# Attention scores from a stacked query by two full-height products, and the second layer's S5 parameter steps started one expert later at a lower rank

## The chip, the cores and the metric

One Trainium2 chip, one core of it. The metric is the time of one execution on the device in microseconds (us); each kernel is run several times and the median is used. The engines are named as in the profile: PE (matrix products and transposes), DVE (vector), ACT (scalar), POOL (GpSimd), and SP, which only issues DMAs here; ACT issues some too.

## What is computed

Two layers of a hybrid backbone on a latent stream of 512 tokens and a context of 256, width 1024. Each layer is a mixer of four branches (attention, SSD, S5, short convolution), merged by gates, and then a mixture of 16 experts in which every expert picks its tokens (64 of the latent stream, 32 of the context). The second layer returns the latent stream alone. The two places that the change touches:

```
def gqa_attend(q, k, v):              # 8 query heads, 2 key heads, head size 64
    qg = q.reshape(b, T, G, H // G, d)
    s = jnp.einsum('btgrd,bsgd->bgrts', qg, k) * (d ** -0.5)
    p = jax.nn.softmax(s, axis=-1)
    o = jnp.einsum('bgrts,bsgd->btgrd', p, v)

def s5_discretise(lam_re, lam_im, log_step, b_re, b_im):
    step = jnp.exp(log_step)[:, None]
    mag = jnp.exp(lr * step)
    ab_re, ab_im = mag * jnp.cos(li * step), mag * jnp.sin(li * step)
    ...
    bb_re = coef_re[..., None] * br - coef_im[..., None] * bi
```

The S5 parameters of a layer (powers of the complex transition, and from them small matrices per group of channels) depend on weights alone, not on the tokens.

## The kernel before, in words

The program is written stage by stage; a scheduler puts each engine's instructions in one fixed order by estimated times and by a priority that follows the order of the code. Each engine then runs its own list strictly in that order, and waits where an operand or a buffer isn't ready.

**Precision.** Many products are made from pairs: `split_to` (L113 to L115) writes a float32 array as a rounded high part (ACT, L114) and a remainder (DVE, L115), and `mm3` (L99 to L101) adds three products: high by high, low by high, high by low.

**Attention** (L861 on). For k and for two groups of four query heads, a projection of 256 columns is made, rotated and normalised into `R` (128 tokens, tile, head, 64). Then `R` is transposed by PE (L925): two query heads side by side make a block of 128 columns, so one transpose serves two heads; a key head is first copied twice side by side into `kd` by DVE (L921). The results go to the pairs `qT` and `kT` (H and L), in which head 0 of a pair holds rows 0 to 63 and head 1 rows 64 to 127. `scores` (L929) runs once for each tile of 128 tokens and each of four head pairs: for two pieces of 384 keys and two heads one `mm3` of 64 rows, that is 12 products, into banks `psb` (three of the four) and `psa`; then maximum (DVE), exponential (ACT, L949) and scaling. `values` transposes the probabilities (L963) and multiplies by V (L968). In the first layer the two context tiles take part too, with one piece of 256 keys. The scheduler fills PE between these with products `psmm` of other stages (gates, modulation), which are due later anyway.

**Experts** (L1500 to L1660). Tokens are gathered by DMA (`xg`), transposed (PE, L1493), scaled (DVE, L1497) and shifted (POOL, L1498) into `X`; one `X0` serves two experts in turn for the latent stream, `X1` the context. For each expert: gate and up products into `psa` (L1507), hidden activation (ACT L1520, DVE L1521 and L1522), its transposes (PE L1525, ACT L1527), down product (L1539), and the weighting `y` (DVE, L1544). What was weighted is split and added to `x` by two more products (L1623, L1625). Weights come in pieces of 1 MB (`we`) by SP.

**The S5 parameters of layer two** are made inside the first layer's experts: `s5_params` (L999) is a generator of some 39 steps, and `up` takes one step at its k equal 1, so four for each expert, from the first expert on. Six steps make tables `T` (DVE, L990 to L995), each written out by a DMA that ACT issues; six groups of four steps follow, each with `Bx` (DVE), its transposes (PE L1123) and copies `Bt` (ACT L1124), `Cx` (DVE, negated in part by ACT, L1129, and written by two DMAs, L1131), and the products `kf` (PE L1141) with copies `KK` (L1145 to L1149). Buffers are shared by tags: `T`, `Bt` and `KK` have one (`out`), `Bx` and `Cx` one (`big`), so a step waits until the DMA of an earlier one has read it.

Of the kernel before, what the change touches and what calls it, by code (L numbers as in the profile page):

```python
# [9 lines left out]
F32 = mybir.dt.float32  # L10
F32R = mybir.dt.float32r
# [34 lines left out]
_PS5 = {}  # L46
# [4 lines left out]
NPS5 = _n  # L51
# [7 lines left out]
class Kern:  # L59
# [799 lines left out]
    def attention(self):  # L859
# [1 line left out]
        V = nc.vector  # L861
        cs, l = self.cst, self.l
        q0 = self.tiles[0] * 128
        qT = [wp.tile([128, 4, 768 - q0], F32R, name="qT" + p) for p in "HL"]
        kT = [wp.tile([128, 2, 768], F32R, name="kT" + p) for p in "HL"]
        Vt = wp.tile([128, NT, 128], F32, name="Vt")
        with self.pool("rope") as rp:
# [14 lines left out]
            for nm, m, c in (("k", 0, C_K), ("q", 0, C_Q), ("q", 1, C_Q + 256)):  # L882
# [29 lines left out]
                Rv = R[:, t0:t0 + tn].rearrange("p t h c -> p (t h) c")  # L912
                V.tensor_mul(Rv, Rv, rq[:, t0:t0 + tn].rearrange("p a b -> p (a b)")[:, :, None].to_broadcast([128, nh * tn, 64]))
                for o, n in (self.streams if nm == "q" else [(256, 512), (0, 256)]):
                    for g in range(2):
                        ps = self.va(n)
                        for i in range(n // 128):
                            t = o // 128 + i
                            if nm == "k":
                                kd = rp.tile([128, 2, 64], F32, name="kd", bufs=2)  # L920
                                V.tensor_copy(kd, R[:, t, g][:, None, :].to_broadcast([128, 2, 64]))  # L921
                                src = kd
                            else:
                                src = R[:, t, 2 * g:2 * g + 2]
                            nc.tensor.transpose(ps[:, i * 128:(i + 1) * 128], src.rearrange("p a c -> p (a c)"), self.ident)  # L925
                        self.split_to(*(z[:, 2 * m + g, o - q0:o - q0 + n] if nm == "q" else z[:, g, o:o + n] for z in (qT if nm == "q" else kT)), ps)
# [72 lines left out]
    def s5_params(self, l, pool):  # L999
# [5 lines left out]
        sm = lambda nm, *s, tag=None: pool.tile([128, *(s or (24,))], F32, name="s5" + nm, tag="s5" + (tag or nm))  # L1005
        p5 = sm("p5", NPS5 - 384)
        Q.dma_start(p5, I["ps5"][l, :, 384:])
        pr = {k: p5[:, a - 384:b - 384] for k, (a, b) in _PS5.items()}

        step, mag, ang = sm("step"), sm("mag"), sm("ang")  # L1010
# [4 lines left out]
        t, sn, cn, rho = sm("t"), sm("sn"), sm("cn"), sm("rho")  # L1015
# [13 lines left out]
        V.tensor_mul(rho, rho, rho)  # L1029
        Q.dma_start(self.s5r[l], rho)  # L1030
        yield
        x1 = sm("x1", 8, 24)

        def powers(P, first, last):

# [6 lines left out]
                a *= 2  # L1042


        un, lo, hi = sm("un", 2, 9, 24), sm("lo", 2, 17, 24, tag="big"), sm("hi", 2, 6, 24)
        V.tensor_copy(un[:, 0, 1], cn)
        V.tensor_copy(un[:, 1, 1], sn)
        for a in (1, 2, 4):
# [11 lines left out]

        for c in range(6):
            gg = slice(4 * c, 4 * c + 4)
            T, e1 = sm("T", 2, 4, 6, 16, tag="out"), sm("e1", 4, 6, 16, tag="e1")
            h4 = lambda i: hi[:, i, :, gg].rearrange("p a g -> p g a")[:, :, :, None].to_broadcast([128, 4, 6, 16])
            l4 = lambda i: lo[:, i, 1:17, gg].rearrange("p a g -> p g a")[:, :, None, :].to_broadcast([128, 4, 6, 16])
            self.cmul(V, T[:, 0], T[:, 1], h4(0), h4(1), l4(0), l4(1), e1)
            Q.dma_start(out[c][:, 2560:], T.rearrange("p i g a b -> p (i g a b)"))
            yield
        pw = sm("pw", 2, 9, 24, tag="un")
# [4 lines left out]
        powers(pw, 1, 8)  # L1074
        yield

        nr, den, cr, ci = sm("nr"), sm("den"), sm("cr"), sm("ci")
# [13 lines left out]
        V.tensor_mul(ci, ci, den)  # L1091
        yield

        PB, PC = sm("PB", 2, 8, 24), sm("PC", 2, 10, 24, tag="hi")
        V.memset(PC, 0.0)
        for s in range(8):
            V.tensor_copy(PB[0:64, :, s], pw[0:64, :, 7 - s])
# [2 lines left out]
        for k in range(9):  # L1100
            V.tensor_copy(PC[64:128, :, 9 - k], pw[64:128, :, k])
        yield
        bb = [sm(f"bb{i}", 5, 16) for i in range(2)]
        for b in bb:
            V.memset(b[:, 4], 0.0)
        cc = [v3(pr["cr"]), v3(pr["ci"])]
        for c in range(6):
# [4 lines left out]
            e1 = sm("e1", 4, 10, 16)  # L1112
            self.cmul(V, bb[0][:, :4], bb[1][:, :4], bc(cr), bc(ci), v3(pr["br"])[:, gg], v3(pr["bi"])[:, gg], e1[:, :, 0])
            Bx = sm("Bx", 2, 4, 8, 16, tag="big")
            ap = lambda P, n, i: P[:, i, :, gg].rearrange("p s g -> p g s")[:, :, :, None].to_broadcast([128, 4, n, 16])
            av = lambda v, n: v[:, :, None, :].to_broadcast([128, 4, n, 16])
            self.cmul(V, Bx[:, 0], Bx[:, 1], ap(PB, 8, 0), ap(PB, 8, 1), av(bb[0][:, :4], 8), av(bb[1][:, :4], 8), e1[:, :, :8])
            yield
            Bt = sm("Bt", 2, 4, 128, tag="out")
            for i in range(2):  # L1120
                ps = self.pa(512)
                for q in range(4):
                    nc.tensor.transpose(ps[:, q * 128:(q + 1) * 128], Bx[:, i, q].rearrange("p s i -> p (s i)"), self.ident)  # L1123
# [3 lines left out]
            Cx = sm("Cx", 2, 4, 10, 16, tag="big")  # L1127
            self.cmul(V, Cx[:, 0], Cx[:, 1], ap(PC, 10, 0), ap(PC, 10, 1), av(cc[0][:, gg], 10), av(cc[1][:, gg], 10), e1)
            nc.scalar.mul(Cx[:, 1], Cx[:, 1], -1.0)  # L1129
            for i in range(2):  # L1130
                Q.dma_start(out[c][:, 1024 + 512 * i:1536 + 512 * i].rearrange("p (g s j) -> p g (s j)", g=4, s=8),  # L1131
                            Cx[:, i, :, 1:9].rearrange("p g s j -> p g (s j)"))
            yield

            KK = sm("KK", 4, 15, 16, tag="out")[:16]
            kf = [self.pa(128).rearrange("p (d j) -> p d j", d=8) for _ in range(2)]
            for d in range(2):
                r = slice(d * 64, d * 64 + 64)
                for q in range(4):
                    for i in range(2):  # L1140
                        nc.tensor.matmul(kf[d][32 * q:32 * q + 32], bb[i][r, q:q + 2].rearrange("p g i -> p (g i)"),  # L1141
                                         Cx[r, i, q, 2 * d:2 * d + 8], start=i == 0, stop=i == 1, skip_group_check=True)
# [282 lines left out]
    def experts(self, l, mp, slotT, io, m5):  # L1425
# [3 lines left out]
        with self.pool("gat", side="right") as gp, self.pool("exp", side="right") as wp, ExitStack() as es:  # L1429
# [71 lines left out]
            def up(w, X, ps, job, e, side):  # L1501
# [304 lines left out]
```

## Time and profile before

| | us |
|---|---|
| three runs | 3124.32, 3130.27, 3125.06 |
| median | 3125.06 |
| the profiled execution | 3127.88 |
| its span | 3126.0 |
| PE busy | 2857.1 (91%) |
| DVE busy | 1615.0 (52%) |
| ACT busy | 790.0 (25%) |
| POOL busy | 444.5 (14%) |

The span is the time from the first to the last instruction of the profiled execution. Shares are averages over stages with different limits: first layer's mixer until about 1130, its experts until about 1800, second mixer until about 2600, its experts to the end. Attention lies at about 600 to 860 and 2220 to 2410.

### The profile page before, as it was taken

Reading aid. Unit: us, or ns where it says so; the run is one execution under the profiler, and the core shown is the slowest. Engines: PE = TensorE matmul, PEld = TensorE weight load, DVE = VectorE, ACT = ScalarE, POOL = GpSimd, SP = SyncE. Lnnn points to the kernel's source line nnn. Section 1 sums busy time; section 2 is a strip of 40 time slices with the busy share of each in tenths; the row PEclk is TensorE's granted clock in tenths of the full one; section 3 lists DMA queues with packets and bytes.
Section 4 is the critical chain, followed back from the end, with each engine's and each line's share of the span. In section 5 each row is a group of like instructions: output and inputs, shape, how many; then the busy total and the mean of one; then the engine's idle time right before and its main releaser. Section 6 shows DMA issues by size and latency. Waiting matters only on the chain. (4 is left out here: it accounts for less than half of the span.)

```text
span 3126.0 us, 47474 instructions
## 1 busy us (share of the span) xinstructions
PE 2857.1 (91%) x18866; PEld 1850.2 (59%) x18866; DVE 1615.0 (52%) x3681; ACT 790.0 (25%) x1733; POOL 444.5 (14%) x551
## 2 busy tenths in 40 slices
PE   7999878999999976999999979999999996998887
PEld 4866756787788952444444448577777884332223
DVE  5477688655326676354522264767654365232223
ACT  4253222425422210011100033321445221000001
POOL 1022265100004120000010010400000031010001
PEclk9999989999999988999999989999999998999999
DMA  7324424311247357898998663255312576999997
GB/s 234 114 67 132 141 86 126 121 48 35 98 156 226 123 204 290 346 344 330 352 372 332 235 210 98 63 167 199 98 44 80 199 265 256 409 409 409 409 409 301
DMA packets 328832, 667.18 MB, mean 213 GB/s; under 512 B 22177, under 2 KB 197537, under 8 KB 327842
## 3 DMA queue, kind: packets, MB, share of 16 engines
q1 hardware_dynamic: 297712, 610.31, 54.4%
q10 hardware_dynamic: 27378, 43.18, 3.8%
q0 software_dynamic: 3520, 10.65, 0.9%
q8 instruction: 149, 2.44, 0.3%
q14 instruction: 73, 0.60, 0.1%
HBM read 609.94 MB, written 52.56 MB: 212 GB/s over the span
## 5 line engine op out<-in xcount | busy, mean ns | idle before, releaser
L1507 PE MATMUL psa<-we,X 128*64 128x512 f32 (+1 forms) x4096 | 593.2, 492 | 49.1 <-DMA we<-in_w_exp_gate_dram 18.3
L1507 PEld LDWEIGHTS psa<-we,X 128*64 128x64 f32 (+1 forms) x4096 | 202.5, 124 | 406.3 <-issue 279.1
L99 PE MATMUL psmm<-hH,fwH 128*128 128x512 f32 x984 | 369.9, 376 | 6.8 <-DVE xpad L632 3.6
L101 PE MATMUL psmm<-hH,fwL 128*128 128x512 f32 x984 | 365.1, 371 | 0.0
L100 PE MATMUL psmm<-hL,fwH 128*128 128x512 f32 x984 | 363.9, 370 | 0.0
L1539 PE MATMUL psa<-we,hidT 128*64 128x512 f32 x992 | 243.9, 611 | 16.1 <-ACT hidT L1527 11.1
L99 PEld LDWEIGHTS psmm<-hH,fwH 128*128 128x128 f32 x984 | 188.1, 191 | 51.7 <-issue 15.3
L101 PEld LDWEIGHTS psmm<-hH,fwL 128*128 128x128 f32 x984 | 188.1, 191 | 33.0 <-issue 6.7
L100 PEld LDWEIGHTS psmm<-hL,fwH 128*128 128x128 f32 x984 | 188.3, 191 | 31.5 <-issue 6.3
L1520 ACT ACTIVATE hid<-psa 128x512 f32<-128x512 f32 (+1 forms) x48 | 25.3, 527 | 605.4 <-PE psa L1507 442.7
L115 DVE TENSOR_TENSOR fwL<-fr,fwH 128x1024 fp32r<-128x1024 f32 (+1 forms) x100 | 109.6, 1097 | 124.0 <-ACT fwH L114 113.4
L1539 PEld LDWEIGHTS psa<-we,hidT 128*64 128x64 f32 x992 | 70.9, 139 | 159.4 <-issue 121.3
L1544 DVE SCALAR_TENSOR_TENSOR y<-psa,ag,m 64x512 f32<-64x512 f32 x62 | 46.5, 749 | 224.6 <-PE psa L1539 223.9
L1498 POOL TENSOR_TENSOR X<-X,modT 128x512 f32<-128x512 f32 x40 | 41.5, 1050 | 697.2 <-DVE X L1497 694.5
L469 POOL TENSOR_TENSOR merged<-merged,tgm 128x512 f32<-128x512 f32 (+1 forms) x48 | 62.5, 1321 | 516.8 <-DMA y<-ys 274.4
L99 PE MATMUL psa<-cwH,hH 128*128 128x256 f32 (+1 forms) x432 | 122.4, 284 | 1.7 <-DVE dtv L697 1.6
L114 ACT CAST fwH<-fr 128x1024 fp32r<-128x1024 f32 (+1 forms) x100 | 89.4, 895 | 132.2 <-PE psmm L100 70.0
L101 PE MATMUL psa<-cwH,hL 128*128 128x256 f32 (+1 forms) x432 | 121.6, 282 | 0.0
L100 PE MATMUL psa<-cwL,hH 128*128 128x256 f32 (+1 forms) x432 | 121.4, 281 | 0.0
L1522 DVE TENSOR_TENSOR hid<-hid,psa 128x512 f32<-128x512 f32 (+1 forms) x48 | 28.7, 597 | 176.7 <-PE psa L1507 176.4
L1521 DVE SCALAR_TENSOR_TENSOR hid<-hid,psa 128x512 f32<-128x512 f32 (+1 forms) x48 | 28.7, 598 | 144.4 <-ACT hid L1520 144.3
L414 ACT ACTIVATE tg<-psmm 128x512 f32<-128x512 f32 x96 | 50.9, 530 | 202.1 <-PE psmm L101 202.0
(645 smaller groups left out, 5860.6 us busy)
## 6 DMA issues: line engine op xcount, KB each, us to landing
we<-in_w_exp_gate_dram SPq DMA_DIRECT2D x128, 1024.0 KB, 8.7
we<-in_w_exp_up_dram SPq DMA_DIRECT2D x128, 1024.0 KB, 13.8
we<-in_w_exp_down_dram SPq DMA_DIRECT2D x128, 1024.0 KB, 15.1
fr<-in_w_mod_dram SPq DMA_DIRECT2D x96, 512.0 KB, 6.5
fr<-in_w_in_dram SPq DMA_DIRECT2D x64, 512.0 KB, 4.2
raw<-in_w_in_dram SPq DMA_DIRECT2D x36, 512.0 KB, 4.0
gs<-tg ACTq DMA_DIRECT2D x32, 384.0 KB, 2.8
tgm<-gs SPq DMA_DIRECT2D x32, 384.0 KB, 3.3
```

What stands on the lines that cost most here:

```text
L99: self.nc.tensor.matmul(ps, ah, bh, start=start and i == 0, stop=False)
L100: self.nc.tensor.matmul(ps, ah, bl, start=False, stop=False)
L101: self.nc.tensor.matmul(ps, al, bh, start=False, stop=stop and i == n - 1)
L114: self.nc.scalar.copy(h, x)
L115: self.nc.vector.tensor_sub(l, x, h.bitcast(F32))
L414: nc.scalar.activation(tg[:, o:o + n], self.cm(w, m, o, n), AF.Tanh, scale=0.5)
L469: (V if i == 3 else nc.gpsimd).tensor_add(dst, dst, t)
L1498: nc.gpsimd.tensor_add(X[:, hk], X[:, hk], Bm[:, 24 + h * 4:28 + h * 4, s:s + 1].to_broadcast([128, 4, 128]))
L1507: self.lastup = nc.tensor.matmul(ps[s][j * c:(j + 1) * c], X[s][:, k, r:r + c], w(k)[:, j * n:(j + 1) * n], start=k == 0, stop=k == 7, ski ...
L1521: V.scalar_tensor_tensor(hid, hid, 1.0, g, op0=OP.add, op1=OP.mult)
L1539: nc.tensor.matmul(ps[j * c:(j + 1) * c], lh, w(k)[:, j * n:(j + 1) * n], start=k == 0, stop=k == 7, skip_group_check=True)
L1544: V.scalar_tensor_tensor(Y[s][r, nn], ps[j * c:(j + 1) * c], got[s][1][r, e:e + 1], m5[s][r, nn], op0=OP.mult, op1=OP.mult)
```

## The change

1. Scores. Every query head is now doubled side by side like a key head, by a POOL copy `kd` with three buffers (k's copies move from DVE to POOL too), and has a transpose of its own. `qS` holds the rounded query in rows 0 to 63 and its remainder in rows 64 to 127; `kT` has the key head twice, as before. One product of 128 rows with `kT` high gives both terms with the high key, a second with `kT` low gives the rest: 8 products for a tile and head pair in place of 12.
2. S5. The buffers are laid out by hand with the same sharing for layer two (`out` for T, Bt and KK; `c0` and `c1` for the two halves of Bx and Cx); the parameters are loaded by two DMAs. The branch for the first layer isn't called.
3. `up` calls `advance` for experts after the first only, and the step is written at a priority 600 lower in rank.

```
-        qT = [wp.tile([128, 4, 768 - q0], F32R, name="qT" + p) for p in "HL"]
+        qS = wp.tile([128, 8, 768 - q0], F32R, name="qS")
...
-                    for g in range(2):
+                    for g in range(nh):
                         ps = self.va(n)
                         for i in range(n // 128):
...
-                            if nm == "k":
-                                kd = rp.tile([128, 2, 64], F32, name="kd", bufs=2)
-                                V.tensor_copy(kd, R[:, t, g][:, None, :].to_broadcast([128, 2, 64]))
+                            kd = rp.tile([128, 2, 64], F32, name="kd", bufs=3)
+                            nc.gpsimd.tensor_copy(kd, R[:, o // 128 + i, g][:, None, :].to_broadcast([128, 2, 64]))
+                            nc.tensor.transpose(ps[:, i * 128:(i + 1) * 128], kd.rearrange("p a c -> p (a c)"), self.ident)
...
+                            z = qS[:, 4 * m + g, o - q0:o - q0 + n]
+                            nc.scalar.copy(z, ps)
+                            V.tensor_sub(z[64:], ps[64:], z[64:].bitcast(F32))
...
-            for i in range(np_):
-                for hh in range(2):
-                    q2, k2 = ([z[R2[hh], hp, tk] for z in qT], [z[R2[hh], hp // 2, i * pn:(i + 1) * pn] for z in kT])
-                    self.mm3(sc[i][hh], [(*q2, *k2)])
+            for hh in range(2):
+                for i in range(np_):
+                    for z in range(2):
+                        nc.tensor.matmul(sc[i][hh], qS[:, 2 * hp + hh, tk], kT[z][:, hp // 2, i * pn:(i + 1) * pn], start=z == 0, stop=z == 1)
...
+    def advance(self):
+
+        p = self.tc.cur_priority
+        self.tc.cur_priority = p + 600
+        next(self.ahead, None)
+        self.tc.cur_priority = p
...
-                    if k == 1:
-                        next(self.ahead, None)
+                    if k == 1 and e:
+                        self.advance()
```

How the order of the instructions moves, at three places. Between the eighth and the ninth expert (`psb_14030` is the end of the eighth expert's down product, `psa_14085` the ninth's gate), PE before:

```order
L1493 MATMUL psmm_13959<-cst_60,xg0_13361 128x128 x4
L1493 MATMUL psmm_13966<-cst_60,xg0_13361 128x128
...
L1539 MATMUL psa_14011<-we_14003,hidT0_13947 64x512 x3
...
L1539 MATMUL psb_14030<-we_14009,hidT1_13956 32x256 x8
L1507 MATMUL psa_14085<-we_14088,X0_13958 64x512 x4
```

And PE now (`psb_13977` the end of the down product, `psa_14032` the gate):

```order
L1574 MATMUL psb_13977<-we_13956,hidT1_13903 32x256 x8
L1151 MATMUL psmm_13416<-cst_60,s5c1_11904 128x128 x3
...
L1151 MATMUL psmm_13713<-cst_60,s5c0_11903 128x128 x4
L1151 MATMUL psmm_13719<-cst_60,s5c1_11904 128x128 x4
...
L1528 MATMUL psmm_13906<-cst_60,xg0_13318 128x128 x4
...
L1528 MATMUL psmm_13913<-cst_60,xg0_13318 128x128 x4
L1542 MATMUL psa_14032<-we_14035,X0_13905 64x512 x3
```

The transposes of the next tokens stood ahead of the down product; now they stand behind it, and behind the transposes and products of two S5 groups. DVE now, at the same place (`y1` reads the end of the down product; rows with `c0`, `c1`, `sm` and `e1` are S5's):

```order
L1579 SCALAR_TENSOR_TENSOR y1_12753<-psb_13977,ag1_11820,m51_11546 32x256 x4
L994 TENSOR_TENSOR s5c1_11904<-s5hi_11907,s5pb_11902 128x640
L996 TENSOR_TENSOR s5c1_11904<-s5c1_11904,s5e1_11906 128x640
...
L994 TENSOR_TENSOR s5c1_11904<-s5PB_11909,s5sm_11910 128x512
L995 TENSOR_TENSOR s5e1_11906<-s5PB_11909,s5sm_11910 128x512
L991 TENSOR_TENSOR s5c0_11903<-s5hi_11907,s5pb_11902 128x640
...
L996 TENSOR_TENSOR s5c1_11904<-s5c1_11904,s5e1_11906 128x640
L992 TENSOR_TENSOR s5e1_11906<-s5sm_11910,s5pa_11901 128x64
L1532 TENSOR_TENSOR X0_13905<-psmm_13906,a_ffn0_6998 128x512
...
L991 TENSOR_TENSOR s5c0_11903<-s5PB_11909,s5sm_11910 128x512
L1532 TENSOR_TENSOR X0_13905<-psmm_13913,a_ffn0_6998 128x512
```

The rest of one S5 group and all of the next stand between the weighting of the eighth expert and the `X0` of the ninth; before, that `X0` (`X0_13958`) stood in DVE's list ahead of the eighth expert's `y0`. Third, the transposes of four query heads in the second layer's attention, PE before:

```order
L925 MATMUL psa_19136<-cst_60,R_18976 128x128 x4
L925 MATMUL psa_19143<-cst_60,R_18976 128x128 x4
```

and now the first nine of sixteen:

```order
L921 MATMUL psa_19146<-cst_60,kd_19147 128x128
L921 MATMUL psa_19146<-cst_60,kd_19150 128x128
L921 MATMUL psa_19146<-cst_60,kd_19153 128x128
L101 MATMUL psmm_21825<-hH_16210,fwL_21815 128x512
L921 MATMUL psa_19146<-cst_60,kd_19156 128x128
L921 MATMUL psa_19161<-cst_60,kd_19162 128x128
L921 MATMUL psa_19161<-cst_60,kd_19165 128x128
L99 MATMUL psmm_21825<-hH_16210,fwH_21814 128x512
L921 MATMUL psa_19161<-cst_60,kd_19168 128x128
L921 MATMUL psa_19161<-cst_60,kd_19171 128x128
L921 MATMUL psa_19176<-cst_60,kd_19177 128x128
```

Each transpose now waits for a POOL copy of its own, and one filling product stands after about three of them. Around the second expert DVE's list keeps its order: there the S5 steps of the tables `T` still stand between the two operations of the hidden activation.

## Rows read from the trace of the kernel before

**Rows 1.** Windows: busy us by engine, PEclk, DMA share; experts 1, attention 2

```profile
core 0: us, PE busy (x) PEld busy (x) DVE busy (x) ACT busy (x) POOL busy (x), PEclk, DMA share, GB/s
1130.00:1800.00 670.00, 624.22 (x5200) 260.67 (x5201) 297.05 (x652) 72.25 (x163) 52.14 (x60) 0.96 0.85 322
2220.00:2410.00 190.00, 188.40 (x1294) 145.21 (x1293) 108.53 (x318) 90.01 (x242) 8.73 (x12) 1.00 0.15 47
```

**Rows 2.** Timeline of PE, one iteration of the second attention (start, duration, both us)

```profile
2302.46 0.44 PE L99 MATMUL psa<-kTH,qTH 64*128 64x384 f32 x1
2302.74 0.34 PE L100 MATMUL psa<-kTL,qTH 64*128 64x384 f32 x1
2302.92 0.33 PE L101 MATMUL psa<-kTH,qTL 64*128 64x384 f32 x1
2303.18 0.87 PE L963 MATMUL psa<-cst,P 128*128 128x128 f32 x6
2303.81 0.48 PE L99 MATMUL psmm<-hH,fwH 128*128 128x512 f32 x1
...
2305.33 0.44 PE L99 MATMUL psb<-kTH,qTH 64*128 64x384 f32 x1
...
2306.21 0.44 PE L99 MATMUL psb<-kTH,qTH 64*128 64x384 f32 x1
...
2306.94 0.44 PE L963 MATMUL psa<-cst,P 128*128 128x128 f32 x2
...
2312.65 0.44 PE L99 MATMUL psb<-kTH,qTH 64*128 64x384 f32 x1
```

**Rows 3.** Timeline of PE, three filling products in a row

```profile
2001.25 0.40 PE L100 MATMUL psmm<-hL,fwH 128*128 128x512 f32 x1
2001.49 0.39 PE L101 MATMUL psmm<-hH,fwL 128*128 128x512 f32 x1
```

**Rows 4.** Groups of POOL by form: busy us, mean ns, idle before

```profile
L1498 POOL TENSOR_TENSOR X<-X,modT 128x512 f32<-128x512 f32 x40 | 41.5, 1050 | 697.2 <-DVE X L1497 694.5 <-DVE xi L1477 2.5
L811 POOL TENSOR_TENSOR S<-S,E 128x128 f32<-128x128 f32 x40 | 21.8, 546 | 83.3 <-DVE S L810 79.8 <-PE psmm L101 1.2 <-DVE rs_y L126 1.1
L908 POOL TENSOR_TENSOR R<-R,tp 128x128 f32<-128x128 f32 x8 | 5.7, 708 | 90.0 <-issue 47.5 <-DVE tp L907 37.0 <-DVE rs_v L124 5.4
L1468 POOL COPY pick<-identb 16x128 bf16<-16x128 bf16 x20 | 6.2, 321 | 121.3 <-PE psmm L1470 119.7 <-PE psmm L101 1.6
```

**Rows 5.** Waits of PE in the first layer's experts: total us, times, longest

```profile
PE psb L1525 <- DVE hid L1522: 16.3, 5, 5.3
PE psa L1507 <- DVE hid L1521: 12.8, 1, 12.8
PE psa L1507 <- POOL X L1498: 1.1, 1, 1.1
```

**Rows 6.** Timeline of PE and DVE, first layer's experts: waits at S5 steps, in brackets

```profile
1474.67 0.67 PE L1525 MATMUL psb<-cst,hid 128*128 128x128 f32 x3 [4.86 <-DVE hid L1522]
1196.70 1.12 DVE L990 TENSOR_TENSOR s5T<-s5hi,s5lo 128x384 f32<-128x384 f32 x1 [5.63 <-DMA s5w<-s5T]
```

**Rows 7.** The tile s5Cx: duration ns min/median/max; landing; wait

```profile
L1129 ACT ACTIVATE s5Cx<-s5Cx x6: 736/736/737, 1333.5 to 1541.6; 128x640 f32<-128x640 f32 x6
DMA to landing us min/median/max: 11.2/12.9/14.5
  DVE s5Bx L990: 8.8, 2
```

**Rows 8.** Groups of DVE by form, first layer's experts: busy us, mean ns

```profile
L1544 DVE SCALAR_TENSOR_TENSOR y<-psb,ag,m 32x256 f32<-32x256 f32 x64 | 30.8, 480 | 21.2 <-PE psb L1539 20.4
L1497 DVE TENSOR_TENSOR X<-psmm,a_ffn 128x512 f32<-128x512 f32 x24 | 16.0, 685 | 6.6 <-PE psmm L1493 6.6
L993 DVE TENSOR_TENSOR s5Cx<-s5PC,s5p 128x640 f32<-128x640 f32 x6 | 4.9, 819 | 0.0
L992 DVE TENSOR_TENSOR s5Bx<-s5Bx,s5e 128x512 f32<-128x512 f32 x6 | 4.1, 679 | 0.0
```

More of the change, by code (lines that the diff above doesn't have):

```diff
@@ L1004, in s5_params, with at, small, bank @@
         v3 = lambda a: a.rearrange("p (g i) -> p g i", g=24)
[L1005 to L1010, printed above, removed]
+        E = V if l else nc.gpsimd
+        place = {}
+        if l:
+            for nm, n in (("pa", 840), ("pb", 768), ("c0", 816), ("c1", 640), ("out", 1024), ("e1", 640), ("hi", 480), ("un", 432), ("PB", 384), ("sm", 616)):
+                place[nm] = pool.tile([128, n], F32, name="s5" + nm)
+        else:
+            for i, nm in enumerate(("pa", "c0", "c1", "e1", "hi", "un", "PB", "sm", "out")):
+                tag = ("fwH", "fwL", "fr")[i // 3]
+                place[nm] = pool.tile([128, 1024], F32, name="s5" + nm, tag=tag, bufs=3)
+            place["pb"] = pool.tile([128, 768], F32, name="s5pb", tag="tg", bufs=2)
+        used = [0]
+        def at(nm, *shape, o=0):
+            n = int(np.prod(shape))
+            ax = "abcd"[:len(shape)]
+            return place[nm][:, o:o + n].rearrange(f"p ({' '.join(ax)}) -> p {' '.join(ax)}", **dict(zip(ax, shape)))
+        def small(*shape):
+            shape = shape or (24,)
+            used[0] += int(np.prod(shape))
+            return at("sm", *shape, o=used[0] - int(np.prod(shape)))
+        def bank(n):
+            return self.pa(n) if l else self.va(n, "b")
+        pr = {}
+        for nm, o, n in (("pa", 384, 840), ("pb", 1224, 768)):
+            Q.dma_start(place[nm][:, :n], I["ps5"][l, :, o:o + n])
+            pr.update({k: place[nm][:, c - o:d - o] for k, (c, d) in _PS5.items() if o <= c < o + n})
+        step, mag, ang = (small() for _ in range(3))
         nc.scalar.activation(step, pr["ls"], AF.Exp)
@@ L1014, in s5_params @@
         V.tensor_mul(ang, pr["li"], step)
-        t, sn, cn, rho = sm("t"), sm("sn"), sm("cn"), sm("rho")
+        t, sn, cn, rho = (small() for _ in range(4))
         M = 12582912.0
@@ L1031, in s5_params @@
         yield
-        x1 = sm("x1", 8, 24)
+        x1 = small(8, 24)
         def powers(P, first, last):
@@ L1042, in powers @@
                 a *= 2
-        un, lo, hi = sm("un", 2, 9, 24), sm("lo", 2, 17, 24, tag="big"), sm("hi", 2, 6, 24)
+        un, lo, hi = at("un", 2, 9, 24), at("c0", 2, 17, 24), at("hi", 2, 6, 24)
         V.tensor_copy(un[:, 0, 1], cn)
@@ L1062, in s5_params @@
             gg = slice(4 * c, 4 * c + 4)
-            T, e1 = sm("T", 2, 4, 6, 16, tag="out"), sm("e1", 4, 6, 16, tag="e1")
+            T, e1 = [at("out", 4, 6, 16, o=i * 384) for i in range(2)], at("e1", 4, 6, 16)
             h4 = lambda i: hi[:, i, :, gg].rearrange("p a g -> p g a")[:, :, :, None].to_broadcast([128, 4, 6, 16])
             l4 = lambda i: lo[:, i, 1:17, gg].rearrange("p a g -> p g a")[:, :, None, :].to_broadcast([128, 4, 6, 16])
-            self.cmul(V, T[:, 0], T[:, 1], h4(0), h4(1), l4(0), l4(1), e1)
-            Q.dma_start(out[c][:, 2560:], T.rearrange("p i g a b -> p (i g a b)"))
+            self.cmul(E, T[0], T[1], h4(0), h4(1), l4(0), l4(1), e1)
+            Q.dma_start(out[c][:, 2560:], place["out"][:, :768])
             yield
-        pw = sm("pw", 2, 9, 24, tag="un")
+        pw = at("un", 2, 9, 24)
         V.memset(pw[:, 0, 0], 1.0)
@@ L1075, in s5_params @@
         yield
-        nr, den, cr, ci = sm("nr"), sm("den"), sm("cr"), sm("ci")
+        nr, den, cr, ci = (small() for _ in range(4))
         ni = pw[:, 1, 1]
@@ L1092, in s5_params @@
         yield
-        PB, PC = sm("PB", 2, 8, 24), sm("PC", 2, 10, 24, tag="hi")
+        PB, PC = at("PB", 2, 8, 24), at("hi", 2, 10, 24)
         V.memset(PC, 0.0)
@@ L1102, in s5_params @@
         yield
-        bb = [sm(f"bb{i}", 5, 16) for i in range(2)]
+        bb = [small(5, 16) for i in range(2)]
         for b in bb:
@@ L1111, in s5_params @@
             bc = lambda a: a[:, gg, None].to_broadcast([128, 4, 16])
-            e1 = sm("e1", 4, 10, 16)
-            self.cmul(V, bb[0][:, :4], bb[1][:, :4], bc(cr), bc(ci), v3(pr["br"])[:, gg], v3(pr["bi"])[:, gg], e1[:, :, 0])
-            Bx = sm("Bx", 2, 4, 8, 16, tag="big")
+            e1 = at("e1", 4, 10, 16)
+            self.cmul(V, bb[0][:, :4], bb[1][:, :4], bc(cr), bc(ci), v3(pr["br"])[:, gg], v3(pr["bi"])[:, gg], at("e1", 4, 16))
+            Bx = [at(f"c{i}", 4, 8, 16) for i in range(2)]
             ap = lambda P, n, i: P[:, i, :, gg].rearrange("p s g -> p g s")[:, :, :, None].to_broadcast([128, 4, n, 16])
             av = lambda v, n: v[:, :, None, :].to_broadcast([128, 4, n, 16])
-            self.cmul(V, Bx[:, 0], Bx[:, 1], ap(PB, 8, 0), ap(PB, 8, 1), av(bb[0][:, :4], 8), av(bb[1][:, :4], 8), e1[:, :, :8])
+            self.cmul(E, Bx[0], Bx[1], ap(PB, 8, 0), ap(PB, 8, 1), av(bb[0][:, :4], 8), av(bb[1][:, :4], 8), at("e1", 4, 8, 16))
             yield
-            Bt = sm("Bt", 2, 4, 128, tag="out")
+            Bt = at("out", 2, 4, 128)
             for i in range(2):
-                ps = self.pa(512)
+                ps = bank(512)
                 for q in range(4):
-                    nc.tensor.transpose(ps[:, q * 128:(q + 1) * 128], Bx[:, i, q].rearrange("p s i -> p (s i)"), self.ident)
+                    nc.tensor.transpose(ps[:, q * 128:(q + 1) * 128], Bx[i][:, q].rearrange("p s i -> p (s i)"), self.ident)
                 nc.scalar.copy(Bt[:, i].rearrange("p a b -> p (a b)"), ps)
@@ L1126, in s5_params @@
             yield
-            Cx = sm("Cx", 2, 4, 10, 16, tag="big")
-            self.cmul(V, Cx[:, 0], Cx[:, 1], ap(PC, 10, 0), ap(PC, 10, 1), av(cc[0][:, gg], 10), av(cc[1][:, gg], 10), e1)
-            nc.scalar.mul(Cx[:, 1], Cx[:, 1], -1.0)
+            Cx = [at(f"c{i}", 4, 10, 16) for i in range(2)]
+            self.cmul(E, Cx[0], Cx[1], ap(PC, 10, 0), ap(PC, 10, 1), av(cc[0][:, gg], 10), av(cc[1][:, gg], 10), e1)
+            nc.scalar.mul(Cx[1], Cx[1], -1.0)
             for i in range(2):
                 Q.dma_start(out[c][:, 1024 + 512 * i:1536 + 512 * i].rearrange("p (g s j) -> p g (s j)", g=4, s=8),
-                            Cx[:, i, :, 1:9].rearrange("p g s j -> p g (s j)"))
+                            Cx[i][:, :, 1:9].rearrange("p g s j -> p g (s j)"))
             yield
-            KK = sm("KK", 4, 15, 16, tag="out")[:16]
-            kf = [self.pa(128).rearrange("p (d j) -> p d j", d=8) for _ in range(2)]
+            KK = at("out", 4, 15, 16)[:16]
+            kf = [bank(128).rearrange("p (d j) -> p d j", d=8) for _ in range(2)]
             for d in range(2):
@@ L1141, in s5_params @@
                         nc.tensor.matmul(kf[d][32 * q:32 * q + 32], bb[i][r, q:q + 2].rearrange("p g i -> p (g i)"),
-                                         Cx[r, i, q, 2 * d:2 * d + 8], start=i == 0, stop=i == 1, skip_group_check=True)
+                                         Cx[i][r, q, 2 * d:2 * d + 8], start=i == 0, stop=i == 1, skip_group_check=True)
             for q in range(4):
```

9 lines of the change are left out of this document (3 added, 6 removed).

## The prediction, made before the changed kernel had run

> **What bounds the kernel now.** I read the busy shares by stage first. In the first layer's experts PE is busy 624 of 670 us while the DMA engines are at 0.85 [rows 1], and in the second attention 188.4 of 190 us: in both PE is the bound, so a microsecond that PE gains or stalls there passes to the end, since the stages follow one another. The reader is to see next, in PE's timeline, what an iteration of attention is made of [rows 2]; then what PE waited for among the experts [rows 5]: some 29 us on the hidden activation (DVE), 1.1 us in all on the next tokens `X`. The third view is why DVE was late: its S5 steps wait for a DMA that reads a shared buffer [rows 6, 7], and what stands behind them on DVE waits too.
>
> **The scores.** One iteration lasts 7.3 us (2305.33 to 2312.65) [rows 2]. Its 12 products take, start to start, 0.88 us (the first six), 0.73 us (2306.21 to 2306.94) and 0.72 us (the last three, by those at 2302.46): 2.33 us. The 8 new ones are of full height and 384 columns. Products of 512 columns follow each other in 0.24 us in a dense stretch [rows 3], so 0.18 us each and 1.4 us for eight. That is the lower end. The upper end is four isolated pairs: an isolated product of the triple took 0.28 us as the first and 0.26 us as the last [rows 2], so 0.54 us a pair and 2.2 us. In the new order the pairs stand between filling products of the same kind, which is nearer to the dense row; I take 1.5 us, a gain of 0.8 us in each of 32 full iterations (four tiles, four head pairs, two layers), 26 us. The eight context iterations go from six to four products of 256 columns; at 0.12 us (half of 0.24) that is 2 us. Bounds of both: 5 to 32 us.
>
> Rows and a rule of the Trainium skill differ here. The first six products, three on the upper and three on the lower 64 rows, took 0.88 us where two lone triples took 1.45 [rows 2]: products of different halves do overlap, but only where two triples follow each other, and two of four triples in an iteration stand alone. The Trainium skill, TensorE: Matmul & The Clock Gate, section "Part 3: Packing small matmuls — row/col tiling", says that matmuls of small height placed in different row groups run at the same time. If that held for all twelve, they would cost six times 0.18 us, less than the new eight, and the change would lose 0.35 us an iteration; the rows say 2.33 us, and I go by them.
>
> **The transposes.** Each query head now has its own: 40 more in both layers together. Six transposes take 0.63 us (2303.18 to 2303.81) [rows 2], 0.105 us each: 4 us lost.
>
> **The doubled heads.** 104 POOL copies (12 and 48 in the first layer, 12 and 32 in the second) now stand before as many transposes, with three buffers. In the new order three transposes come between two filling products of some 0.24 us, so PE wants a copy every 0.2 us or so. No row shows this copy. Nearest below is a POOL copy of as many elements on 16 partitions, 0.32 us; above, an addition of the same shape, 0.55 us in one place and 0.71 us in attention [rows 4]. I take 0.40 us, nearer the copy. With hand-over 0.06 us (my choice), past the first three copies POOL sets the pace: in the second layer's groups of 16, 13 times 0.46 is 6.0 us against 16 times 0.105 and five fillings of 0.25, 2.9 us; so 3 us lost, less half a us of filling before the first transpose. The groups of 24 in the first layer have more filling and lose 2 us, those of 12 for k some 1.2 us. Two of each: 12 us (6 at 0.32, 35 at 0.71). The ACT and DVE evictions, twice as many, lie beside PE; if they were late, the next bank would be, but the fourth bank of a group waits only for the first's. DVE's 24 key copies, gone, were beside PE as well.
>
> Attention: 26 and 2 gained, 4 and 12 lost: **12 us faster** (25 faster to 34 slower at all ends).
>
> **The S5 steps.** Of the longest stall, 12.8 us on the second expert's hidden activation [rows 5], nothing goes: the tables `T` still stand between that expert's two hidden operations on DVE, and still have one buffer, whose DMA DVE waits for (5.6 us once) [rows 6]. What goes is the later stall of 4.9 us [rows 6] and about 1 us more of the same kind: 6 us faster.
>
> What comes: before, `X0` of the next pair of experts was made ahead of the down product, and PE waited 1.1 us in all for `X` [rows 5]. Now, between the eighth and ninth expert, it stands behind one and a half S5 groups. I follow DVE from the end of the down product, t = 0. `y1`, four pieces of 0.48 us [rows 8]: 2.0. Two `Cx` operations of 0.82 us [rows 8]: 3.7. ACT's negation, 0.74 us [rows 7]: 4.5, and its DMA is issued; it lands 12.9 us later (11.2 to 14.5) [rows 7]: 17.4. The next `Bx` writes the same half, `c1`, and waits for it; DVE did wait for such DMAs before, 8.8 us in two cases [rows 7]. Then three `Bx` operations of 0.68 and six `Cx` of 0.82 [rows 8]: 24.3, and the negation 25.0. The transposes of the next tokens stand on PE behind `kf` products that wait for ACT's copies `Bt` behind that negation, some 1.5 us. `X0`'s first half, 0.69 us on DVE [rows 8] and 1.05 us on POOL [rows 4]: about 29 us before PE begins the gate. The second half stands behind a `Bx` of the group after, which waits for the `c0` DMA issued at 25: 38, and with 0.69, 0.69 and 1.05 us the second half is there at 40. Between, PE has half a gate product, 3.5 us (624 us over 48 expert products [rows 1] is 13 us each with all that lies between, of which I take 7 for the latent stream's), and about 4 us of S5 products and transposes (my choice). So PE stalls about **32 us** there. Should the DMAs land 1.7 us sooner, as the shortest did, it is 29; if the second half's DMA was of the fast kind and landed in 5 us, about 23.
>
> The same pattern costs less at three places. At the tenth expert the gate's activation stands behind a negation on ACT, and the up product behind it: 6 us. At the next pair, `X0` follows `y1` and five `Cx` operations (2.0, 4.1, then 0.69 and 1.05): 8 us. One pair later it follows `y0`, a subtraction and `y1`: 3 us. Together 17 us, less if DVE comes to them early: 8 to 20. The two loads of the parameters in place of one cost nothing; they are covered by the first expert, and if not, by one DMA. SP's weights are ahead of PE in this stage, so they hide no part of the stall.
>
> Experts: 32 and 17 lost, 6 gained: **43 us slower** (25 to 55).
>
> **The sum.** 43 less 12 is 31 us slower, 3159 us against the profiled execution's 3127.88, which lies 2.8 us above the median of 3125.06; against the median 3156. The forecast's own range is 3134 to 3178.
>
> **The rivals.** *No bunching in effect.* If the S5 DMAs land at once when PE stalls (the weight loads then cease for want of buffers), the handovers cost some 14 us in all, the removed stall gives 6 back, and attention's 12 to 25 stay: 3108 to 3121, faster. For it: the DMA share of 0.85 [rows 1] falls when PE stands. Against: the T buffer's wait of 5.6 us fell in a stretch where PE stood too. It decides where the landing is under about 4 us. Chance 0.2, at 3114. *A wash.* Attention at its good end (25) and experts at their low (25): 3125; chance 0.1. *The copies are dear.* If each costs 0.71 us, the loss at the transposes is 35 in place of 12 us, and the total 3179; chance 0.1. For it, POOL's addition of the same shape did take that in attention and 0.55 us elsewhere [rows 4]. The Trainium skill, SBUF — State Buffer, section "Who interferes with whom", says that a VectorE instruction with two SBUF inputs and a GpSimd instruction that reads SBUF exclude each other for the whole instruction; by that the copies would wait for DVE's subtractions. The spread between the two rows agrees with it without proving it. *The steps do leave the first two experts.* Then the early stalls of some 23 us go as well: 3133; the order speaks against it, chance 0.05.
>
> **How the numbers follow.** The forecast has 0.55. A measurement of this kernel tells about 0.2%, 6 us, from no change. Faster by more: the first rival and a little of the wash's, 0.22. Within: 0.12. Slower: 0.66. The range holds the forecast's own and, to leave out no more than 2 in 10, the dear copies in part below 3180 and the faster side down to 3112.
>
> **What would show it.** In the changed profile PE's longest wait among the first layer's experts is on `X` of POOL at the ninth expert, in one or two pieces of some 30 us, where 12.8 us on the hidden activation stays at the second. In attention the eight score products of an iteration take 1.4 to 1.8 us, the POOL copies 0.32 to 0.55 us, and PE waits on them some 12 us. If `X` costs PE under 15 us in all, the second part is wrong; if the second attention grows longer, the first is.

## The result, and the profile after

The changed kernel took 3147.34 us (median of five, 3141.39 to 3152.23) against 3125.06 for the kernel before on the same chip (3115.66 to 3130.27): a ratio of 1.0073, 95% interval 1.0049 to 1.0097. That is slower by 22 us, where 31 had been forecast. The profiled execution has a span of 3144.0 us (3126.0 before).

By stage, the two profiles differ in three places. The rows of the next fence are the first layer's expert products of the kernel before, gate and up, then down, with their first and last start; the fence behind it has the same of the changed kernel.

```profile
L1507 PE MATMUL psa<-we,X x3072: 379/379/1114, 1143.6 to 1783.8; 128*32 128x256 f32 x128, 128*64 128x512 f32 x64
L1539 PE MATMUL psb<-we,hidT x1024: 379/379/403, 1186.7 to 1797.2; 128*32 128x256 f32 x171
```

```profile
L1542 PE MATMUL psa<-we,X x3072: 378/379/1116, 1127.5 to 1808.9; 128*32 128x256 f32 x127, 128*64 128x512 f32 x65
L1574 PE MATMUL psb<-we,hidT x1024: 378/379/405, 1168.8 to 1822.3; 128*32 128x256 f32 x171
```

The first mixer, with the router, ends 16 us earlier (1127.5 for 1143.6). The experts take 694.8 us (1822.3 less 1127.5) for 653.6: 41 us more. The rest is 7 us shorter, which makes the 18 us between the two spans.

What PE waited for among the experts of the changed kernel, in place of [rows 5]: rows of the view of waits from 1100 to 1850 (total us, times, longest) that concern the hidden activation, S5 and `X`:

```profile
PE psa L1542 <- DVE hid L1556: 11.6, 1, 11.6
PE psb L1560 <- DVE hid L1557: 6.3, 2, 6.1
PE psmm L1169 <- ACT s5c L1157: 5.6, 2, 3.8
PE psmm L1169 <- DVE s5c L993: 5.2, 2, 3.5
PE psmm L1151 <- DVE s5c L993: 3.6, 1, 3.6
PE psmm L1151 <- DVE s5c L996: 2.6, 1, 2.6
PE psa L1542 <- POOL X L1533: 2.0, 2, 1.1
PE psmm L1528 <- DVE X L1532: 1.9, 2, 1.0
PE psmm L1505 <- DVE X L1532: 1.2, 1, 1.2
```

The first two are in the main the second expert's stalls, as before. The next four are new, 17.0 us together: PE waits for S5's own results, at its transposes and `kf` products. All waits for the tokens `X`, on POOL and on DVE, come to 5.1 us. PE's timeline at the end of the eighth expert shows the order of it (start, duration; the wait ahead of a row in brackets):

```profile
1454.97 3.66 PE L1574 MATMUL psb<-we,hidT 128*32 128x256 f32 x64
1458.56 0.55 PE L1151 MATMUL psmm<-cst,s5c 128*128 128x128 f32 x3
...
1463.24 1.15 PE L1169 MATMUL psmm<-s5c,s5sm 64*32 64x128 f32 x28 [3.79 <-ACT s5c L1157]
1468.04 1.08 PE L1151 MATMUL psmm<-cst,s5c 128*128 128x128 f32 x4 [3.65 <-DVE s5c L993]
...
1477.02 1.09 PE L1169 MATMUL psmm<-s5c,s5sm 64*32 64x128 f32 x14 [1.85 <-ACT s5c L1157]
...
1479.27 1.11 PE L1528 MATMUL psmm<-cst,xg 128*128 128x128 f32 x4
...
1482.36 3.68 PE L1542 MATMUL psa<-we,X 128*64 128x512 f32 x6
...
1527.05 3.66 PE L1574 MATMUL psb<-we,hidT 128*32 128x256 f32 x64
```

From the end of one down product (1458.6) to the first gate product (1482.4) pass 23.8 us; the ninth expert, from its predecessor's last down product to its own, lasts 72.1 us (1454.97 to 1527.05). Before, the same two rows are 44.2 us apart:

```profile
1487.38 3.66 PE L1539 MATMUL psb<-we,hidT 128*32 128x256 f32 x64
1531.61 3.66 PE L1539 MATMUL psb<-we,hidT 128*32 128x256 f32 x64
```

So 27.9 of the 41 us are there. Part of it is the clock. In the window of the stall PE waits 13.8 us, all at S5's products, and is busy the other 10, at a granted clock of 0.58 (columns as in [rows 1]):

```profile
1458.60:1482.40 23.80, 9.99 (x89) 5.92 (x85) 16.80 (x34) 6.34 (x15) 1.04 (x1) 0.58 0.74 251
```

In the 20 us from 1465 on it is 0.50, the lower of the two levels (1.2 GHz for 2.4); the engine had stood before that, with only short products between.

In attention, a tile and head pair now has eight score products (timeline of PE, where [rows 2] had twelve):

```profile
2343.78 0.34 PE L942 MATMUL psb<-kTH,qS 128*128 128x384 f32 x1
2343.95 0.33 PE L942 MATMUL psb<-kTL,qS 128*128 128x384 f32 x1
2344.12 0.40 PE L99 MATMUL psmm<-hH,fwH 128*128 128x512 f32 x1
...
2349.00 0.44 PE L942 MATMUL psa<-kTH,qS 128*128 128x384 f32 x1
2349.28 0.34 PE L942 MATMUL psa<-kTL,qS 128*128 128x384 f32 x1
2349.46 0.71 PE L964 MATMUL psa<-cst,P 128*128 128x128 f32 x5
```

A pair between filling products takes 0.34 us (2343.78 to 2344.12), one that stands alone 0.46; three of the one and one of the other are 1.48 us, the 1.5 of the prediction. The POOL copies and who waited for them:

```profile
L920 POOL COPY kd<-R x104: 280/293/1287, 612.9 to 2325.0; 128x128 f32<-128x128 f32 x104
  PE psa L921: 6.6, 7
```

### The profile page after: what moved, and what is told of

The parts are those of the page before. It is cut to its first block, busy times and chain, and to the rows that moved or that the text cites. A ratio compares the mean times of both kernels' runs of the same rounds, so it can differ in the third digit from the quotient of the medians.

```text
span 3144.0 us, 47391 instructions
## 1 busy us (share of the span) xinstructions
PE 2859.9 (91%) x18762; PEld 1854.0 (59%) x18762; DVE 1618.1 (51%) x3669; ACT 795.1 (25%) x1745; POOL 479.7 (15%) x655
## 5 line engine op out<-in xcount | busy, mean ns | idle before, releaser
L1542 PE MATMUL psa<-we,X 128*64 128x512 f32 (+1 forms) x4096 | 608.6, 496 | 47.3 <-DMA we<-in_w_exp_gate_dram 18.9
L100 PEld LDWEIGHTS psmm<-hL,fwH 128*128 128x128 f32 x984 | 188.8, 192 | 28.5 <-issue 5.6
```

Source lines behind the costliest of these rows:

```text
L100: self.nc.tensor.matmul(ps, ah, bl, start=False, stop=False)
```

## The experiments

All were timed in five rounds beside the kernel before; its median there was between 3124.9 and 3127.7 us. Expert spans are worked out as above.

**Each part alone.** The first kernel takes the attention of the change and everything else of before; the second the reverse.

> The scores' part of the change alone, the S5 steps as before. Theory (the two parts don't touch each other): 22 to 23 us faster than before, 3102 us; by stage, 16 us in the first mixer, 6 to 7 in the second, the first layer's experts within 1 us of the 654 us that they took before. Rival (the mixers are shorter only since other work was put off into the experts): no faster than 3118, and the experts longer than 660 us.

Measured: 3108.09 us, ratio 0.9949 (0.9934 to 0.9964), 16 us faster (11 to 21): short of the 22 to 23 that I had read off the stages, and not the rival's either.

> The S5 part alone (buffers by hand, begin with the second expert, lower rank), the scores as before. Theory: 41 us slower, 3166 us, all of it in the first layer's experts (695 us in place of 654), the ninth expert near 72 us. Rival (the stall needs the scores' part too, or the mixers give something back): 3145 to 3155.

Measured: 3169.27 us, ratio 1.0142 (1.0122 to 1.0163), 44 us slower; its experts take 698.4 us, the ninth 73.3, as the theory had it. The parts add up: 44 less 16 is 28, for 22 measured, within the intervals. The ends of the first mixer scatter by some us between profiled executions of the same scores (1127.5 to 1134.7), so stage differences there are worth no more than that; the 16 us by which the changed kernel's first mixer ended earlier stand at the favourable end of that. Two rows of the first kernel, like those above, show that with the scores alone the experts kept their length, 654.8 us:

```profile
L1508 PE MATMUL psa<-we,X x3072: 379/379/1113, 1133.4 to 1774.9; 128*32 128x256 f32 x128, 128*64 128x512 f32 x64
L1540 PE MATMUL psb<-we,hidT x1024: 379/379/403, 1175.9 to 1788.2; 128*32 128x256 f32 x171
```

**The S5 part taken apart.** First the whole change without the later begin and the rank; then with the later begin, but without the 600:

```
-                    if k == 1 and e:
-                        self.advance()
+                    if k == 1:
+                        next(self.ahead, None)
```

> The whole change but for the begin and the rank: one step for each up from the first expert on, at the common rank, with the new buffers. Theory (begin and rank cost, the buffers don't): as the scores alone, 3102 us within 5; experts of the first layer 650 to 658 us. Rival (the buffers laid out by hand add waits that bunch the steps): 3120 or more.

Measured: 3094.85 us, ratio 0.9908 (0.9890 to 0.9926): 13 us less than the scores alone. Neither theory had this; the buffers gain. The experts take 643.3 us:

```profile
L1542 PE MATMUL psa<-we,X x3072: 379/379/1117, 1129.7 to 1759.6; 128*32 128x256 f32 x128, 128*64 128x512 f32 x64
L1574 PE MATMUL psb<-we,hidT x1024: 379/379/403, 1170.6 to 1773.0; 128*32 128x256 f32 x171
```

```
-        self.tc.cur_priority = p + 600
+        self.tc.cur_priority = p
```

> The change with the begin at the second expert but no lower rank. In its order some 14 S5 operations of DVE stand between the hidden activation and the next tokens at four experts, but still ahead of the down product's end. Theory (the rank is what costs, the later begin little): 3105 to 3120 us, no expert but the second over 55 us. Rival (the later begin is what costs): 3140 to 3150, with one expert near 70 us.

Measured: 3173.95 us, ratio 1.0156 (1.0141 to 1.0172), slower still than the change, and above what theory and rival had. No expert reached 70 us, but four beside the second lay between 55 and 61. The edit had left a thing in: after a step, `advance` sets the rank counter back, so what follows shares the ranks of the step. Here that made no block of S5 steps, but the opposite: at the sixth expert PE's list takes two products of S5 and two of gate or up in turn, sixteen times over. Below are the end of this in PE's timeline, and the window of the sixth expert, first here and then in the kernel with the steps in line (columns as in [rows 1]):

```profile
1384.02 0.40 PE L1169 MATMUL psmm<-s5c,s5sm 64*32 64x128 f32 x2
1384.35 0.62 PE L1542 MATMUL psa<-we,X 128*32 128x256 f32 x2
1384.90 0.40 PE L1169 MATMUL psmm<-s5c,s5sm 64*32 64x128 f32 x2
1385.23 3.23 PE L1542 MATMUL psa<-we,X 128*32 128x256 f32 x56
```

```profile
1351.00:1410.00 59.00, 54.55 (x359) 19.26 (x353) 22.56 (x44) 8.03 (x19) 5.45 (x5) 0.97 0.68 252
```

```profile
1351.00:1388.00 37.00, 37.00 (x357) 15.03 (x347) 17.42 (x37) 6.39 (x16) 4.29 (x5) 1.00 0.82 303
```

A round of two and two takes 0.88 us (1384.02 to 1384.90), where 56 such gate or up products without S5 between them take 3.16, 0.11 for two. PE is busy nearly all the time, 54.6 of 59 us, with about as many products as it did there in 37. So most of this kernel's loss isn't waiting behind a block: PE's own work took longer when it was mixed so finely. The next kernel has the later begin without `advance`:

```
-                    if k == 1 and e:
-                        self.advance()
+                    if k == 1 and e:
+                        next(self.ahead, None)
```

> Scores and buffers of the change, steps from the second expert on, but taken in line as before: no lower rank and no setting back of the rank counter after a step (which the last run still had). Theory (what bunches the steps is the rank, set back or lowered; the later begin costs nothing): 3095 us within 5, no expert but the second over 50 us. Rival (the later begin by itself bunches them): 3140 to 3175.

Measured: 3094.36 us, ratio 0.9896 (0.9881 to 0.9911), the same as from the first expert on. The later begin costs nothing, and what separates this kernel from the change is `advance` alone: 53 us. About half of that is PE standing still: over the whole program PE is busy 2859.9 us in the changed kernel and 2833.8 here, with the same number of products, so 26 of the 50 us between the two spans are products that take longer (at the lower clock, and in another order; the two aren't separated). Last, the rank without the later begin:

```
-                    if k == 1 and e:
+                    if k == 1:
                         self.advance()
```

> The whole change, but with steps from the first expert on (lower rank kept). In its order 22 and 5 S5 operations of DVE stand ahead of the tokens of the seventh or ninth expert. Theory (the rank bunches, whatever the begin): 3135 to 3160 us, one expert near 70 us. Rival (rank only hurts together with the later begin): 3090 to 3110.

Measured: 3138.49 us, ratio 1.0041 (1.0027 to 1.0055), 44 us over the same without `advance`; the ninth expert is the long one here too, 65.6 us:

```profile
1475.63 3.66 PE L1574 MATMUL psb<-we,hidT 128*32 128x256 f32 x64
1541.28 3.66 PE L1574 MATMUL psb<-we,hidT 128*32 128x256 f32 x64
```

**Where the stall sits.** The prediction had put it on `X0`'s place in DVE's list. Here `X` leaves DVE and POOL:

```
+                    if l == 0:
+                        for q in range(4):
+                            k = h * 4 + q
+                            nc.scalar.activation(X[:, k], ps[:, q], AF.Identity, scale=A[:, k, s:s + 1], bias=Bm[:, 24 + k, s:s + 1])
+                        continue
```

> The whole change, but in the first layer the next tokens X are scaled and shifted by ACT in one operation for each 128 columns, so X stands no longer in DVE's list behind the S5 operations; PE's list still has the transposes of those tokens behind the S5 transposes and products of two groups. Theory A (PE's list sets the stall: the tokens' transposes wait behind S5 products that wait for DVE and ACT): the ninth expert stays at 62 us or more and the total at 3135 to 3150. Theory B (the place of X in DVE's list sets it, as the prediction put it): the ninth expert falls below 52 us and the total below 3130.

Measured: 3139.18 us, ratio 1.0046 (1.0033 to 1.0060). The ninth expert stays at 73.8 us (1460.27 to 1534.12), and the waits stand at the same S5 products; the gate begins 2 us behind the first of the tokens' transposes (PE's timeline):

```profile
1468.54 1.15 PE L1169 MATMUL psmm<-s5c,s5sm 64*32 64x128 f32 x28 [3.79 <-ACT s5c L1157]
1474.88 1.09 PE L1151 MATMUL psmm<-cst,s5c 128*128 128x128 f32 x4 [5.19 <-DVE s5c L993]
...
1485.21 1.11 PE L1528 MATMUL psmm<-cst,xg 128*128 128x128 f32 x4
...
1487.26 3.67 PE L1547 MATMUL psa<-we,X 128*64 128x512 f32 x6
```

So theory A: PE's own list holds the ninth expert, with the tokens' transposes behind S5 products that wait for DVE and ACT. (A kernel with those transposes ahead of the S5 products in PE's list wasn't run.) The experts together are 6.5 us shorter than in the change, above all the second and the thirteenth.

**What the buffers gain.** The buffers of before, but `Bx` and `Cx` each as two tiles with a buffer for each half; scores as in the change:

```
-            Bx = sm("Bx", 2, 4, 8, 16, tag="big")
+            Bx = [sm(f"Bx{i}", 4, 8, 16, tag=f"big{i}") for i in range(2)]
...
-            Cx = sm("Cx", 2, 4, 10, 16, tag="big")
+            Cx = [sm(f"Cx{i}", 4, 10, 16, tag=f"big{i}") for i in range(2)]
```

> The scores' part alone, with the buffers of before, but the two halves of Bx and Cx as tiles of their own, so that a half of the next Bx waits for the DMA of its own half only. Theory (this is what the buffers of the change gain: the stalls of 6.0 and 2.1 us in the middle experts go, and the early ones stay): 3095 to 3101 us, experts 643 to 649 us. Rival (the gain is in other buffers, such as the shared scratch or the small tables): 3106 to 3110, experts 652 us or more.

Measured: 3090.95 us, ratio 0.9883 (0.9866 to 0.9899). That is all of the buffers' gain, and a little more than expected; against the scores alone the eighth expert is 9 us shorter and the tenth 4. In the kernel with the scores alone, DVE waited for both halves' DMAs, then six operations of `Bx` and one of `Cx` stood ahead of the hidden activation; in this one the wait is shorter and comes inside (DVE's timelines, scores alone first):

```profile
1455.26 0.69 DVE L991 TENSOR_TENSOR s5Bx<-s5PB,s5bb 128x512 f32<-128x512 f32 x1 [7.44 <-DMA s5w<-s5Cx]
...
1460.83 0.69 DVE L1523 TENSOR_TENSOR hid<-hid,psa 128x512 f32<-128x512 f32 x1
```

```profile
1442.13 0.67 DVE L991 TENSOR_TENSOR s5Bx<-s5PB,s5bb 128x512 f32<-128x512 f32 x1
...
1445.73 0.69 DVE L994 TENSOR_TENSOR s5Bx<-s5PB,s5bb 128x512 f32<-128x512 f32 x1 [0.87 <-DMA s5w<-s5Cx]
```

PE's waits for the hidden activation `hid` (DVE, two lines) fall from 28.5 to 19.3 us, again scores alone first:

```profile
PE psb L1526 <- DVE hid L1523: 16.3, 5, 5.9
PE psa L1508 <- DVE hid L1522: 12.2, 1, 12.2
```

```profile
PE psa L1508 <- DVE hid L1522: 10.6, 1, 10.6
PE psb L1526 <- DVE hid L1523: 8.7, 3, 3.7
```

**The second expert's stall.** Two buffers for the tables `T`, with the buffers of the change (`c1` made long enough for a table) and steps in line:

```
-            T, e1 = [at("out", 4, 6, 16, o=i * 384) for i in range(2)], at("e1", 4, 6, 16)
+            tb = "c1" if c % 2 else "out"
+            T, e1 = [at(tb, 4, 6, 16, o=i * 384) for i in range(2)], at("e1", 4, 6, 16)
...
-            Q.dma_start(out[c][:, 2560:], place["out"][:, :768])
+            Q.dma_start(out[c][:, 2560:], place[tb][:, :768])
```

> Scores and buffers of the change, steps in line from the first expert, and the six tables T written in turn from two buffers (out and c1) in place of one. Theory (the second expert's stalls of 12.4 and 6.6 us come from DVE's waits for the one buffer's DMA): 8 to 15 us less than with one buffer, 3080 to 3087 us. Rival (they come from DVE's own T operations ahead of the hidden activation): 3091 to 3097.

Measured: 3087.58 us, ratio 0.9878 (0.9863 to 0.9893), 7 us less than the two kernels with steps in line and one table buffer. It is the lowest median of all, though its interval overlaps that of the halves alone (3090.95). The 6.6 us stall is gone, 9.6 of 12.4 us are left. With halves as tiles instead, the same edit:

```
-            T, e1 = sm("T", 2, 4, 6, 16, tag="out"), sm("e1", 4, 6, 16, tag="e1")
+            T, e1 = sm("T", 2, 4, 6, 16, tag="big1" if c % 2 else "out"), sm("e1", 4, 6, 16, tag="e1")
```

> The last kernel with the tables T in turn in two buffers (out and the second half's). Theory (as with the change's buffers, where this gave 7 us): 3082 to 3087 us, the second expert near 47 us. Rival (the second expert's 10.6 us stall stays, since DVE's own T operations fill the time): 3089 to 3094.

Measured: 3090.15 us, ratio 0.9889 (0.9872 to 0.9905): no gain over 3090.95 that can be told; the second expert's stall is still there, 12.7 us. And with `X` by ACT, the edit of "Where the stall sits", on top of the fastest:

> The fastest so far (scores and buffers of the change, steps in line, two table buffers) with X by ACT as in the run before. Theory (DVE's S5 operations ahead of X and the hidden activation of the second expert still cost 9.6 us there, and X is off DVE now): 2 to 8 us less, 3080 to 3086 us. Rival (X isn't waited for in this order): 3086 to 3091.

Measured: 3090.78 us, ratio 0.9893 (0.9876 to 0.9910): no gain either, as the rival said. What is left of the stall is DVE's own work: in the 9.6 us before PE goes on (at 1200.38 in the kernel with two table buffers), DVE waits 0.5 us for a DMA and is otherwise busy with S5's tables and powers, ahead of the hidden activation in its list.

**The copies' buffers.** Scores and buffers of the change, steps in line:

```
-                            kd = rp.tile([128, 2, 64], F32, name="kd", bufs=3)
+                            kd = rp.tile([128, 2, 64], F32, name="kd", bufs=8)
```

> Scores and buffers of the change, steps in line from the first expert, and eight buffers for the doubled heads in place of three. Theory (PE's 6.6 us of waits for POOL's copies are mostly the three buffers' turn-around): 3 to 6 us less, 3089 to 3092 us. Rival (POOL's 0.29 us a copy against PE's 0.1 us a transpose sets the pace in any case): the same waits, 3094 to 3096.

Measured: 3093.34 us, ratio 0.9890 (0.9875 to 0.9905); PE's waits for the copies went from 6.6 to 5.8 us. The time lies between theory and rival and decides nothing; the waits, of which seven eighths stay, speak for the rival: not the number of buffers but POOL's pace sets most of them.

## Why the prediction was right, point by point

**Direction, size and range.** Right: 3147 lies in the likeliest case's own range, 3134 to 3178, and 22 of 31 us came. Errors of opposite sign helped: `advance` cost 53 us where 49 had been summed, the buffers gave 13 for 6 and attention 16 for 12. The terms, as the prediction put them:

- *Scores, 26 and 2 us gained.* The product times were right (1.5 us for eight). The whole part gained 16 us alone (11 to 21) where 12 had been summed. Mis-sized was the copy: 0.29 us for the 0.40 taken, below even the 0.32 of the lower row, so PE waits 6.6 us for the 12 summed. With 6.6 the sum would be 17; what is left is noise.
- *The good end of attention, 25.* By its own terms (32 less 4 less 6) it is 22, and the low end of the ninth expert's stall comes to 25 by the steps given, not 23; neither changes the forecast.
- *The rule on row groups*, had it held for all twelve products, would have had the change lose 0.35 us an iteration; it gained 0.85. The Trainium skill, TensorE: Matmul & The Clock Gate, "Part 3: Packing small matmuls — row/col tiling", says that small products in different row groups run at the same time. The trace agrees with it where two triples met, 0.88 us for both; a triple that stood alone took 0.73 or 0.72 [rows 2].
- *The tables' stall stays.* Right: 11.6 and 6.1 us are there at the second expert.
- *A later stall goes, 6 us.* It does, but it needs neither the rank nor the begin: with the separate halves of `Bx` and `Cx` it goes with the steps in line too, and the buffers gain about 13 us. The description of the change calls them the same sharing, and the prediction gave them no term of their own; that step failed.
- *Ninth expert 32 us, then 6, 8 and 3.* Against the kernel that differs by `advance` alone, the ninth lasts 72.1 for 44.2 us: 28. The tenth, eleventh and thirteenth are 5, 10 and 12 us longer, the seventh 4 shorter; the sum over all experts is 51 for the 49 put down. The thirteenth was sized wrong, 12 for 3. In the windows of the eleventh and thirteenth PE stands only 4 and 2 us; the rest is PE at work, at granted clocks of 0.90 and 0.94. The prediction counted idle time alone.
- *Through `X0`'s place in DVE's list.* This step was wrong. The waits for `X` are 5.1 us in all, and by the prediction's own sentence ("if `X` costs PE under 15 us in all, the second part is wrong") its account of the second part fails, though the size came. The stall stands earlier in PE's list, at the S5 transposes and products ahead of the tokens' transposes, which the order ahead of the prediction did show. With `X` off DVE it stayed.
- *The DMA landing, 12.9 us.* DVE's wait for the `Cx` half that was issued at 1463.2 ended at 1469.0, after 0.9 us of waiting, so it landed in under 6 us; the wait for the half issued from 1476.3 on ended at 1485.9, within 9.6 us. The first rival put its point at 4 us, and that wasn't reached; DVE's own operations (16.8 us busy in those 23.8) filled most of the time besides. Against that rival the prediction had said that DVE's 5.6 us wait for a table's DMA fell where PE stood. It didn't: PE was at work then (from 1190.33, for 7.09 us); the wait that fell into PE's stall is the next one, 4.05 us.

**`advance`, not the begin.** The prediction didn't separate them. The later begin costs nothing; `advance` costs 44 to 53 us. It does two things, it lowers the rank by 600 and sets the counter back after the step, and how far each has a part is open: no run has the 600 without the setting back, and the setting back alone makes another order, with products finely mixed, slower by some 80 us than plain steps.

**The rivals.** "No bunching in effect", "A wash" and "The steps do leave the first two experts" fell. "The copies are dear" fell at 0.29 us. The kernel with the change's scores and buffers, steps in line and two table buffers is faster than both the kernel before and the change: 3087.58 us.

## What to carry to other kernels

In this kernel, work off the critical path cost least in pieces of middle size, each at a place where its operands were ready. Taken in line, 32 S5 products stood in one piece of 0.7 us inside an expert and PE hardly waited. With a rank 600 lower and the counter set back, the steps were put off until two groups stood in one block between two experts, in PE's list as well as in DVE's; why the scheduler placed them just there isn't shown. Strewn two by two among the gate products they cost more still. Look for such places in the list of the engine that is the bound, not only in that of the engine which is late. And give each half of a result that a DMA writes out a buffer of its own: the next writer's first half then needn't wait for the DMA of the second, which gave 13 to 17 us here.

## What the runs showed that I had not expected

A POOL copy of one float32 input on 128x128 takes 0.29 us at the median, about half of the 0.55 and less than half of the 0.71 us of an addition with two inputs of that shape [rows 4]. A stall costs more than the idle time that the view of waits shows. In the 23.8 us PE waits only 13.8; the rest is work, most of it at the lower clock level, and that goes on behind the stall: six gate products took 3.68 us at 1482.4, and six 1.93 us at 1490.2, when the granted clock was back at 1.00. And the order of PE's list can cost more than the waits do: with the counter set back and no lower rank, PE is busy 64 us longer than with plain steps (2897.5 for 2833.8), of the 80 us lost.
